# An MLP of seven block products: first product in 2 passes of 1024 tokens with stored operands, second without GpSimd in its loop

## The chip, the cores and the metric

One of the eight cores of a Trainium2 chip runs the kernel, one launch for the whole layer. The metric is the device time of one execution in microseconds, as the median over runs; lower is better. The engines are TensorE (PE, with its weight loads as PEld), VectorE (DVE), ScalarE (ACT), GpSimd (POOL) and SyncE (SP), which issues most transfers here.

## What is computed

The reference is one transformer layer over 2048 tokens of width 1024 (attention heads beside RWKV heads, an output projection, LayerNorm, then an MLP). The change lies in the MLP at the end and in what prepares it; cut to that:

```python
D_MODEL = 1024; SEQ = 2048; D_FF = 4 * D_MODEL

def squared_relu_mlp(h, w1, w2):
    return jnp.square(jax.nn.relu(h @ w1)) @ w2

    ...
    y = jnp.concatenate([y_na, y_rw], axis=-1) @ w_out
    x = layer_norm(ALPHA * x + g1 * y, ln1_g, ln1_b)
    x = layer_norm(ALPHA * x + g2 * squared_relu_mlp(modulate(x, sh2, sc2), mlp_w1, mlp_w2), ln2_g, ln2_b)
```

All values are float32.

## The kernel before

`phase1` and the first part of `tail` compute the two head groups; nothing changes there. Then come four stretches of `tail`.

**Opening.** `out_tiles` computes the output projection in 16 tiles of 128 tokens, with the first LayerNorm (`norm1`), and stores rows to X1 and their normalised form to XN in memory. The loop over the last tiles also calls `xstep`, which prepares the token side of the first product: it loads rows of XN (L1362), transposes them on TensorE (L1372), modulates them on ScalarE (L1375), forms block sums on VectorE (L1377 to L1380), and splits the result into a high part rounded to fp32r on ScalarE (L1382) and a low part on GpSimd (L1383). A step covers one of 4 slices of the width; four steps make the operands of 512 tokens. All steps use one tile `uk`.

**Split products.** A float32 product is taken as three fp32r products (high x high, high x low, low x high), so each operand is split into a rounded copy (ScalarE) and a rest (a subtraction, VectorE or GpSimd). On top of that a 2 x 2 block product is computed with 7 block products instead of 8, from sums of blocks. The 7 are numbered; products 1, 6, 7 and 4 of a group add up in one PSUM bank (a), 5 and 3 in another (b), 2 in a third.

**First product** (`mlp1`). Four passes of 512 tokens, the blocks being 256 tokens, 512 of the width and 128 hidden columns. A pass runs over 16 groups of 256 hidden columns, with 1 MB of weights per group loaded in each pass. A product is 12 matmuls of 256 columns (L1469). `prep` makes the weight side four products ahead: block sums (L1419 to L1425), high part (L1428), low part (L1429), all on ScalarE and VectorE. `seq` interleaves the products of two neighbouring groups. Behind the matmuls three results are copied (L1477) and three added to them (L1487); one instruction squares the group's 1024 columns (L1480), and the hidden values go to H in memory. At the end of a pass the operands of the next are split (L1491, L1492); `xstep` has made them during the pass.

**Second product** (`mlp2`). Two halves of 1024 tokens. A half runs over 7 groups of 512 hidden rows by the 7 products, and an eighth group that is computed with plain products. One of its units (a product of a group) is 24 matmuls of 512 columns (L1610). `load` reads H and the weights, `prep` makes block sums of both sides (S at L1550, T at L1557, on GpSimd but for a few at the start of a half) and `split` their parts (L1530: tokens on VectorE, weights on GpSimd or VectorE). Units are prepared two ahead. After each unit its four banks are added to `acc` (L1617; L1615 is the first copy). `std_prep` prepares the eighth group (GpSimd multiplies and splits its weights), and `mlp_end` computes it (L1679, L1681), combines it with X1 (L1662 on GpSimd for 6 of 8 rows, L1663), normalises and stores.

The order on each engine is that of a list scheduler which walks the program by priority of program order and lets later work pass where earlier work is not ready in its own simulation. Tiles share memory by tags with a number of buffers; a new tile waits for the last reader of the one whose place it takes. Pools of a stage that has ended give their memory to the next stage.

Of the kernel before, what the change touches and what calls it, by code (L numbers as in the profile page):

```python
# [15 lines left out]
D = 1024  # L16
# [26 lines left out]
M1LEAD = 4  # L43
M2LEAD = 2
FAST = (1, 5, 6, 3)
# [9 lines left out]
class Kern:  # L55
# [4 lines left out]
    def setup(self):  # L60
# [29 lines left out]
        self.H = scr("H", [32, 128, T])  # L90
# [709 lines left out]
    def tail(self):  # L800
        nc, tc, a = self.nc, self.tc, self.a
        ex = ExitStack()
        with ExitStack() as ep:
            with ExitStack() as eo:
# [57 lines left out]
                self.psN = self.pool(ep, "psN", 4, space=PSUM, side="right")  # L862
                self.xp = self.pool(ex, "xp", 1, side="right")
                self.xh = self.xp.tile([128, 7, 4, 256], F32R, name="xuh")
                self.xl = self.xp.tile([128, 7, 4, 256], F32R, name="xul")
                for i, _ in enumerate(tiles):
                    if i < 2:
                        self.xstep(0, 2 * i)
                        self.xstep(0, 2 * i + 1)
        with ExitStack() as em:  # L870
            self.base = self.pool(em, "base", 4)
            with ExitStack() as e1:
                self.mlp1(e1)
            ex.close()
            self.mlp2(em)

# [479 lines left out]
    def xstep(self, q, k, u=None):  # L1356
        nc = self.nc
        pool = self.xp
        t = pool.tile([128, 4, 2, 128], F32, name="xn", bufs=2)
        for j in range(4):  # L1360
            r = OB[2 * q + j // 2] + j % 2 * 128
            nc.sync.dma_start(t[:, j], self.XN[r:r + 128, :].rearrange("p (x k c) -> p x k c", x=2, c=128)[:, :, k, :])  # L1362
        if u is None:
            uk = pool.tile([128, 7, 256], F32, name="uk")
            at = [uk[:, i] for i in range(7)]
        else:
            at = [u[i // 2][:, i % 2, k * 256:k * 256 + 256] for i in range(7)]
        b12 = pool.tile([128, 256], F32, name="b12")
        for x, ds in enumerate(((at[0], b12), (at[1], at[2]))):
            ps = self.psN.tile([128, 512], F32, name="psn")  # L1370
            for j in range(4):
                nc.tensor.transpose(ps[:, j * 128:(j + 1) * 128], t[:, j, x, :], self.ident)  # L1372
            kk = 4 * x + k
            for c, d in enumerate(ds):
                nc.scalar.activation(d, ps[:, c * 256:c * 256 + 256], AF.Identity, bias=self.m2[:, 0, kk:kk + 1],  # L1375
                                     scale=self.m2[:, 1, kk:kk + 1])
        nc.vector.tensor_tensor(at[3], b12, at[0], ALU.subtract)  # L1377
        nc.vector.tensor_tensor(at[4], at[2], at[3], ALU.subtract)
        nc.vector.tensor_tensor(at[5], at[2], b12, ALU.subtract)
        nc.vector.tensor_tensor(at[6], at[1], at[4], ALU.subtract)  # L1380
        if u is None:
            nc.scalar.copy(self.xh[:, :, k, :], uk)  # L1382
            nc.gpsimd.tensor_tensor(self.xl[:, :, k, :], uk, f32(self.xh[:, :, k, :]), ALU.subtract)  # L1383


    def mlp1(self, es):
        nc, a = self.nc, self.a
        P = lambda name, **kw: self.pool(es, name, 1, **kw)
        up, sp, srcp, zp, pp = P("w1u"), P("w1sum"), P("w1src"), P("h1"), P("h1p")
        lp = P("l1c")  # L1390
# [5 lines left out]
        src, sums, units = {}, {}, {}  # L1396

        def load(g):
            if g < NG:
                if g < 2:  # L1400
                    t = self.base.tile([128, 2, 1024], F32, tag="c8", name="w10")
                    src[g] = t.rearrange("p a (k c) -> p (a k) c", k=4)
                else:
                    src[g] = srcp.tile([128, 8, 256], F32, name="w1", bufs=3)
                c = g % 16 * 256
                (nc.scalar if g < 2 else nc.sync).dma_start(src[g], a["mlp_w1"].rearrange("(k p) c -> p k c", p=128)[:, :, c:c + 256])

        def prep(n):
# [3 lines left out]
            w = src[g]  # L1412
            a11, a12, a21, a22 = [w[:, 4 * k:4 * k + 4, f * 128:f * 128 + 128] for f in range(2) for k in range(2)]
            if pr in (1, 2, 4):
                x = {1: a11, 2: a12, 4: a22}[pr]
            else:
                x = sums[g, pr] = sp.tile([128, 4, 128], F32, name="w1s", bufs=5)
                if pr == 5:
                    nc.vector.tensor_tensor(x, a21, a22, ALU.add)  # L1419
                elif pr == 6:  # L1420
                    nc.vector.tensor_tensor(x, sums.pop((g, 5)), a11, ALU.subtract)
                elif pr == 7:
                    nc.vector.tensor_tensor(x, a11, a21, ALU.subtract)
                else:
                    nc.vector.tensor_tensor(x, a12, sums.pop((g, 6)), ALU.subtract)  # L1425
            h = up.tile([128, 4, 128], F32R, tag="w1u", name="w1h", bufs=20)
            l = up.tile([128, 4, 128], F32R, tag="w1u", name="w1l", bufs=20)
            nc.scalar.copy(h, x)  # L1428
            nc.vector.tensor_tensor(l, x, f32(h), ALU.subtract)  # L1429
# [371 lines left out]
```

## Time and profile before

| | us |
|---|---|
| median of 3 runs | 3548.64 (3531.97 to 3555.44) |
| profiled execution, its own time | 3559.12 |
| its span, first to last instruction | 3557.3 |
| first product, about | 2161 to 2832 |
| second product, about | 2832 to 3557 |

The span is the time between the first and the last instruction of one profiled execution; the time of that execution lies 1.8 us above. Engine busy times are sums over instructions, and matmuls overlap, so TensorE's busy time is above the time that its matmuls occupy it. In a table of stretches PEclk is the share of TensorE's full clock that was granted.

### The profile page before, as it was taken

What the parts mean: (1) busy time and instruction counts of PE and PEld (TensorE: products, weight loads), DVE (VectorE), ACT (ScalarE), POOL (GpSimd) and SP (SyncE); (2) the same over time, 40 slices, a digit from 0 to 9 for tenths busy, and PEclk for the clock granted to TensorE, in tenths of its full rate; (3) what the DMA queues carried; (4) which work ended last, traced back from release to release, by engine and by line L of the source; (5) the groups of instructions that cost most, each with busy time, mean ns of one, the idle gap of its engine ahead of it and who ended that gap; (6) DMA issues with size and microseconds to landing.
All of it is one profiled execution on the core that took longest, in us unless ns stands there. A gap on an engine that the chain in (4) does not pass through costs nothing. (4 is left out here: it accounts for less than half of the span.)

```text
span 3557.3 us, 71137 instructions
## 1 busy us (share of the span) xinstructions
PE 3240.4 (91%) x27864; PEld 2749.8 (77%) x27864; DVE 2903.6 (82%) x5245; ACT 1630.7 (46%) x3201; POOL 1036.4 (29%) x715
## 2 busy tenths in 40 slices
PE   7999999899939988999979988999999999989987
PEld 4878898789836766777757768999999978767775
DVE  5568887879696667776578768999999789999998
ACT  4555565455414445454432123565655443344333
POOL 0000000000014444544343331000000077877785
PEclk9999999899969999999989989999999999999998
DMA  7487367546775555454364535555455423243322
GB/s 245 141 244 206 95 165 193 156 114 173 191 176 127 121 133 122 116 137 109 81 202 154 151 126 198 177 163 169 157 172 197 158 102 117 97 148 113 119 95 83
DMA packets 752291, 528.48 MB, mean 149 GB/s; under 512 B 376940, under 2 KB 671596, under 8 KB 751956
## 3 DMA queue, kind: packets, MB, share of 16 engines
q1 hardware_dynamic: 676586, 487.47, 47.1%
q10 hardware_dynamic: 75370, 36.46, 3.6%
q8 instruction: 220, 3.60, 0.4%
q14 instruction: 115, 0.94, 0.1%
HBM read 359.70 MB, written 164.11 MB: 147 GB/s over the span
## 5 line engine op out<-in xcount | busy, mean ns | idle before, releaser
L442 PE MATMUL psm<-xh,wh 128*128 128x386 f32 (+1 forms) x1104 | 380.4, 347 | 14.5 <-ACT row L445 10.3
L442 PE MATMUL psm<-xl,wh 128*128 128x386 f32 (+1 forms) x1104 | 380.4, 345 | 3.3 <-DVE xl L413 3.2
L442 PE MATMUL psm<-xh,wl 128*128 128x386 f32 (+1 forms) x1104 | 376.5, 341 | 0.0
L1530 POOL TENSOR_TENSOR ul<-wp,uh 128x1024 fp32r<-128x1024 f32 x50 | 142.3, 2850 | 733.2 <-ACT uh L1530 729.6
L1469 PE MATMUL psa<-xuh,w1l 128*128 128x256 f32 x1024 | 287.8, 283 | 9.1 <-DVE w1l L1429 8.9
L1469 PE MATMUL psa<-xuh,w1h 128*128 128x256 f32 x1024 | 290.0, 284 | 4.6 <-ACT p L1477 1.7
L1469 PE MATMUL psa<-xul,w1h 128*128 128x256 f32 x1024 | 288.1, 282 | 0.0
L442 PEld LDWEIGHTS psm<-xh,wh 128*128 128x128 f32 x1104 | 210.0, 191 | 40.7 <-ACT row L445 20.9
L442 PEld LDWEIGHTS psm<-xl,wh 128*128 128x128 f32 x1104 | 210.1, 190 | 17.9 <-issue 7.3
L442 PEld LDWEIGHTS psm<-xh,wl 128*128 128x128 f32 x1104 | 210.1, 190 | 5.0 <-issue 3.7
L1469 PEld LDWEIGHTS psa<-xuh,w1l 128*128 128x128 f32 x1024 | 193.2, 189 | 10.4 <-DVE w1l L1429 10.4
L1469 PEld LDWEIGHTS psa<-xuh,w1h 128*128 128x128 f32 x1024 | 193.8, 189 | 6.8 <-ACT p L1477 2.6
L1469 PEld LDWEIGHTS psa<-xul,w1h 128*128 128x128 f32 x1024 | 193.9, 189 | 0.0
L752 DVE TENSOR_TENSOR stmp<-mp,xp 128x9 f32<-128x9 f32 (+30 forms) x310 | 168.2, 543 | 24.3 <-DMA vw<-VN 7.4
L1428 ACT CAST w1h<-w1s 128x512 fp32r<-128x512 f32 x256 | 156.3, 622 | 67.6 <-PE psa L1469 25.1
L1429 DVE TENSOR_TENSOR w1l<-w1s,w1h 128x512 fp32r<-128x512 f32 x256 | 176.2, 698 | 8.7 <-ACT w1h L1428 8.2
L1610 PE MATMUL psqa<-ul,uh 128*128 128x512 f32 x400 | 162.7, 407 | 20.4 <-DVE ul L1530 18.3
L428 DVE TENSOR_TENSOR wl<-wst,wh 128x1024 fp32r<-128x1024 f32 x81 | 98.7, 1219 | 87.3 <-ACT wh L427 69.4
L1610 PE MATMUL psqa<-uh 128*128 128x512 f32 x400 | 154.1, 401 | 14.0 <-ACT uh L1530 7.2
L982 POOL TENSOR_SCALAR S<-S,mx 128x640 f32<-128x640 f32 (+1 forms) x128 | 106.0, 828 | 202.2 <-DVE mx L980 121.4
L1610 PE MATMUL psqb<-ul,uh 128*128 128x512 f32 x384 | 151.0, 393 | 11.7 <-DVE ul L1530 8.7
L1610 PE MATMUL psqa<-uh,ul 128*128 128x512 f32 x400 | 161.0, 402 | 0.0
(405 smaller groups left out, 10151.0 us busy)
## 6 DMA issues: line engine op xcount, KB each, us to landing
w<-in_mlp_w SPq DMA_DIRECT2D x62, 1024.0 KB
wst<-in_w_in SPq DMA_DIRECT2D x81, 512.0 KB
H<-h SPq DMA_DIRECT2D x64, 512.0 KB
hp<-H SPq DMA_DIRECT2D x32, 1024.0 KB
wp<-in_mlp_w SPq DMA_DIRECT2D x32, 1024.0 KB
wmod<-in_w_mod SPq DMA_DIRECT2D x48, 512.0 KB
bkc<-BK SPq DMA_DIRECT2D x36, 512.0 KB
AR<-ar SPq DMA_DIRECT2D x64, 256.0 KB
```

The source lines that it names most:

```text
L428: nc.vector.tensor_tensor(wl, w, f32(wh), ALU.subtract)
L442: nc.tensor.matmul(ps[:, :y - x], lhsT=s[:, k, :], rhs=m[:, k, x:y], start=(i == 0), stop=(i == 23))
L752: nc.vector.tensor_tensor(tv, mp[:, i:i + 1, lo:lo + n].to_broadcast([128, n, n]), xp[:, lo:lo + n, lo:lo + n], ALU.mult)
L982: nc.gpsimd.tensor_scalar(x, x, m[:, 6:7], 1.0, ALU.mult, ALU.mult)
L1428: nc.scalar.copy(h, x)
L1429: nc.vector.tensor_tensor(l, x, f32(h), ALU.subtract)
L1469: nc.tensor.matmul(ps, lhsT=w[:, k, :], rhs=x[:, xu[pr], k, :], start=(i == 0 and pr in (1, 5, 2)), stop=(i == 11), skip_group_check=True)
L1530: return (h, l), [lambda: nc.scalar.copy(h, x), lambda: eng.tensor_tensor(l, x, f32(h), ALU.subtract)]
L1610: nc.tensor.matmul(ps, lhsT=x[:, c, s], rhs=y[:, c, :], start=(i == 0 and new), stop=(i == 5), skip_group_check=True)
```

## The change

The first product is done in 2 passes of 1024 tokens with blocks of 512, so its matmuls have 512 columns and there are 32 groups; the products of a group run one after the other (`MORD`), the weight side is prepared three products ahead, and each weight block is loaded once per pass. The token operands of a pass are made in 8 steps of `xstep` (4 slices of the width by 2 halves of each token block). Before pass 1 the steps split three operands and store the other four to a buffer XU in memory, from which `mlp1` loads and splits them; the second pass's seven operands are all stored to XU by steps during the first pass and reloaded as the first pass's last group releases each tile. Splits of token operands are on VectorE, none on GpSimd.

After the matmuls `mlp1` squares the four blocks of a group separately, forms the block sums that the second product needs, and stores all seven operands to HU (for the last two blocks of each pass, which belong to the plain group, the four blocks alone). The second product loads one operand per unit, three units before it is prepared, and splits it in place. Weight differences are formed in place on VectorE. Its groups (`M2G`) are two units deep: two consecutive units of one product add up in the same PSUM banks and are then added to `acc` once. `std_prep` runs on VectorE and ScalarE. `mlp_end` itself is not changed.

The diff, cut to its core:

```diff
-M1LEAD = 4
+M1LEAD = 3
 M2LEAD = 2
-FAST = (1, 5, 6, 3)
+ALEAD = 3
+MORD = (1, 5, 6, 3, 7, 2, 4)
+XU = {pr: i for i, pr in enumerate(MORD)}
+M2G = ((0, 2), (4, 2), (8, 2), (12, 1))
+M2STD = 14
-        self.H = scr("H", [32, 128, T])
+        self.HU = scr("HU", [2, 16, 128, 7, 512])
+        self.XU = scr("XU", [2, 128, 7, 4, 512])
...
+                self.uk = self.base.tile([128, 8, 256], F32, tag="uk", name="uk")
...
+                self.w1load(0)
+                m = 0
                 for i, _ in enumerate(tiles):
-                    if i < 2:
-                        self.xstep(0, 2 * i)
-                        self.xstep(0, 2 * i + 1)
+                    for m in range(m, min(m + 3, 8)):
+                        self.xstep(0, m // 2, m % 2)
+                    m += m < 8
...
+    def xstep(self, q, k, c):
...
+        def keep(pr):
+            if q == 0:
+                h, l = self.xu[pr]
+                nc.scalar.copy(h[:, k, cs], x[pr])
+                V.tensor_tensor(l[:, k, cs], x[pr], f32(h[:, k, cs]), ALU.subtract)
...
+        V.tensor_tensor(x[4], x[2], x[6], ALU.subtract)
+        for pr in MORD[:3]:
+            keep(pr)
+        i = 3 if q == 0 else 0
+        nc.sync.dma_start(self.XU[q, :, i:7, k, cs], self.uk[:, i:7])
...
+    def w1load(self, g):
+        if g < 32:
+            pool, tag = (self.xp, "w1a") if g % 2 == 0 else (self.srcp, "w1b")
+            self.w1[g] = pool.tile([128, 8, 256], F32, tag=tag, name="w1")
+            c = g % 16 * 256
+            self.nc.sync.dma_start(self.w1[g], self.a["mlp_w1"].rearrange("(k p) c -> p k c", p=128)[:, :, c:c + 256])
...
     def mlp1(self, es):
-        NG = 64
-        seq = [(g + o, pr) for g in range(NG + 1) for o, pr in ((0, 1), (-1, 7), (0, 5), (-1, 3), (0, 6), (-1, 4), (0, 2))
-               if 0 <= g + o < NG]
+        NG = 32
+        seq = [(g, pr) for g in range(NG) for pr in MORD]
...
+        def xload(q, pr):
+            nc.sync.dma_start(f32(self.xu[pr][1]), self.XU[q, :, XU[pr]])
+        def xsplit(pr, src=None):
+            h, l = self.xu[pr]
+            src = f32(l) if src is None else src
+            nc.scalar.copy(h, src)
+            V.tensor_tensor(l, src, f32(h), ALU.subtract)
+        def square(z):
+            V.scalar_tensor_tensor(z, z, 0.0, z, ALU.max, ALU.mult)
+        for pr in MORD[3:]:
+            xload(0, pr)
+        self.w1load(1)
+        todo = {n + 1: [lambda pr=pr: xsplit(pr)] for n, pr in enumerate(MORD[3:])}
...
+            if g == 15:
+                if pr == 1:
+                    xsplit(1, u1)
+                else:
+                    xload(1, pr)
+                    todo.setdefault(n + 4, []).append(lambda pr=pr: xsplit(pr))
+            def out(z, u, q=q, fg=fg):
+                todo.setdefault(n + 1, []).append(lambda: nc.sync.dma_start(self.HU[q, fg, :, XU[u]], z))
...
+            elif pr == 7:
+                z12, z22 = st["p", 6], st["p", 5]
+                V.tensor_tensor(z22, ps, z22, ALU.add)
+                square(z22)
+                out(z22, 4)
+                if not std:
+                    s = st["s1"] = T("s1")
+                    V.tensor_tensor(s, z12, z22, ALU.add)
+                    out(s, 5)
...
     def mlp2(self, es):
+        def hload(half, fg, pr):
+            t = up.tile([128, 2, 512], F32R, tag="al", name="al", bufs=6)
+            nc.sync.dma_start(f32(t), self.HU[half, fg:fg + 2, :, XU[pr]].rearrange("c p t -> p c t"))
+            return t
...
+        seq = [(half, g, pr, kk) for half in range(2) for g in range(len(M2G)) for pr in MORD for kk in range(M2G[g][1])]
...
+            if y is not None:
+                fs.append(lambda: V.tensor_tensor(B, y, B, ALU.subtract))
+            al = hs.pop(n)
+            ah = u3("ah")
+            ub, fb = split(B)
+            units[n] = (ah, al), ub
+            fs += [lambda: nc.scalar.copy(ah, f32(al)), fb[0],
+                   lambda: V.tensor_tensor(al, f32(al), f32(ah), ALU.subtract), fb[1]]
...
-                new = pr in (1, 5, 2)
+                new = pr in (1, 5, 2) and kk == 0
...
+                if not end:
+                    pass
+                elif g == 0 and pr in (1, 5, 6, 4):
                     nc.scalar.copy(o, ps)
...
-        fs = [lambda w=w: nc.gpsimd.tensor_tensor(w, w, g2[:, None, :].to_broadcast([128, 2, D]), ALU.mult) for w in wp]
+        fs = [lambda w=w: nc.vector.tensor_tensor(w, w, g2[:, None, :].to_broadcast([128, 2, D]), ALU.mult) for w in ws]
```

## Rows read from the trace of the kernel before

**Rows 1.** The page, engine totals: busy time, share of the span, instructions.

```profile
PE 3240.4 (91%) x27864; PEld 2749.8 (77%) x27864; DVE 2903.6 (82%) x5245; ACT 1630.7 (46%) x3201; POOL 1036.4 (29%) x715
```

**Rows 2.** Table of stretches: start to end, length, busy time (and count) per engine.

```profile
core 0: us, PE busy (x) PEld busy (x) DVE busy (x) ACT busy (x) POOL busy (x), PEclk, DMA share, GB/s
2080.00:2160.00 80.00, 72.65 (x299) 53.54 (x297) 61.66 (x94) 23.05 (x41) 31.02 (x15) 0.91 0.36 115
2160.00:2230.00 70.00, 59.47 (x456) 58.27 (x457) 64.09 (x108) 34.83 (x75) 8.46 (x2) 0.90 0.59 201
2230.00:2832.00 602.00, 596.89 (x5014) 593.25 (x5012) 557.79 (x945) 342.62 (x704) 0.00 (x0) 1.00 0.52 169
2832.00:3112.00 280.00, 264.11 (x1126) 212.95 (x1127) 266.08 (x246) 105.73 (x114) 215.75 (x75) 0.98 0.33 117
3112.00:3215.00 103.00, 80.36 (x329) 63.58 (x328) 96.13 (x90) 51.44 (x77) 72.43 (x25) 0.92 0.42 151
3215.00:3478.00 263.00, 249.48 (x1067) 202.89 (x1067) 256.17 (x243) 97.51 (x102) 208.65 (x72) 0.97 0.29 105
3478.00:3558.00 80.00, 53.38 (x219) 42.84 (x217) 69.19 (x77) 24.43 (x41) 44.28 (x15) 0.86 0.20 79
```

**Rows 3.** Chain of waits: start, length, what, in each product.

```profile
2816.24 2.84 PE psa L1469 x24
...
2858.27 5.44 PE psqb L1610 x24
```

**Rows 4.** Table of stretches, matmul line of the first product alone.

```profile
2161.00:2832.00 671.00, 650.75 (x5376) 642.83 (x5376) 0.99 0.53 171
```

**Rows 5.** Second product: tile ul (minimum/median/maximum ns), then groups by line (busy us, mean ns).

```profile
L1530 DVE TENSOR_TENSOR ul<-S,uh x56: 1209/2196/3397, 2839.1 to 3459.3; 128x1024 fp32r<-128x1024 f32 x56
L1530 DVE TENSOR_TENSOR ul<-hp,uh x50: 1208/3052/5039, 2833.4 to 3499.4; 128x1024 fp32r<-128x1024 f32 x50
...
L1617 DVE TENSOR_TENSOR acc<-psqb,acc 128x512 f32<-128x512 f32 x184 | 119.1, 677 | 4.7 <-PE psqb L1610 4.7
```

**Rows 6.** First product: groups by line (busy us, mean ns).

```profile
L1429 DVE TENSOR_TENSOR w1l<-w1s,w1h 128x512 fp32r<-128x512 f32 x256 | 176.2, 698 | 8.7 <-ACT w1h L1428 8.2 <-PE psa L1469 0.2
L1428 ACT CAST w1h<-w 128x512 fp32r<-128x512 f32 x192 | 114.1, 622 | 41.6 <-PE psa L1469 18.0 <-DMA w<-in_mlp_w 16.6 <-PE pse L1469 3.1
...
L1480 DVE SCALAR_TENSOR_TENSOR h<-h 128x1024 f32<-128x1024 f32 x63 | 76.6, 1217 | 5.9 <-ACT h L1479 5.8
...
L1419 DVE TENSOR_TENSOR w1s<-w 128x512 f32<-128x512 f32 x64 | 43.7, 683 | 8.5 <-DMA w<-in_mlp_w 8.5
L1487 DVE TENSOR_TENSOR h<-pse,p 128x256 f32<-128x256 f32 x64 | 26.7, 418 | 9.8 <-ACT w1h L1428 4.0 <-PE pse L1469 3.3 <-ACT p L1477 1.4
```

**Rows 7.** Waits in the second product: us in total, times, longest.

```profile
ACT uh L1530 <- POOL S L1550: 201.3, 49, 7.8
...
PEld psqa L1610 <- DVE ul L1530: 22.8, 11, 4.8
```

**Rows 8.** Start of the first product: one stretch, one row of TensorE's timeline.

```profile
2160.00:2170.00 10.00, 2.40 (x11) 2.19 (x12) 4.29 (x7) 2.55 (x5) 0.00 (x0) 0.67 1.00 349
...
2168.11 0.58 PE L1469 MATMUL psa<-xuh,w1l 128*128 128x256 f32 x1 [6.41 <-DVE w1l L1429]
```

**Rows 9.** Opening: VectorE's timeline, groups of GpSimd and ScalarE, DMA issues (ns).

```profile
2088.18 0.35 DVE L1380 TENSOR_TENSOR uk<-uk 128x256 f32<-128x256 f32 x1
...
2130.34 0.41 DVE L1380 TENSOR_TENSOR uk<-uk 128x256 f32<-128x256 f32 x1
...
L1383 POOL TENSOR_TENSOR xul<-uk,xuh 128x1792 fp32r<-128x1792 f32 x4 | 16.2, 4050 | 36.9 <-ACT xuh L1382 36.9
...
L1375 ACT ACTIVATE u<-psn,m 128x256 f32<-128x256 f32 x36 | 19.3, 564 | 7.5 <-PE psn L1372 7.2
...
L1362 SPq DMA_DIRECT2D xn<-XN x64: 517/605/1222, 2070.6 to 2526.0; - x64
```

**Rows 10.** Last matmuls: first and last start of a line (us).

```profile
L1679 PE MATMUL psqb<-uh,ul x64: 388/389/389, 3146.6 to 3537.6; 128*128 128x512 f32 x64
```

More of the change, by code (lines that the diff above doesn't have):

```diff
@@ L1376, in xstep @@
                                      scale=self.m2[:, 1, kk:kk + 1])
[L1377 to L1383, printed above, removed]
+        V.tensor_tensor(x[5], at[7], x[1], ALU.subtract)
@@ L1408, in prep @@
+        seq = [(g, pr) for g in range(NG) for pr in MORD]
+        sums, units = {}, {}
         def prep(n):
@@ L1411, in prep @@
             g, pr = seq[n]
-            w = src[g]
+            w = self.w1[g]
             a11, a12, a21, a22 = [w[:, 4 * k:4 * k + 4, f * 128:f * 128 + 128] for f in range(2) for k in range(2)]
-            if pr in (1, 2, 4):
-                x = {1: a11, 2: a12, 4: a22}[pr]
[L1416 to L1425, printed above, removed]
@@ L1428, in prep @@
+            h = up.tile([128, 4, 128], F32R, tag="w1u", name="w1h", bufs=10)
+            l = up.tile([128, 4, 128], F32R, tag="w1u", name="w1l", bufs=10)
             nc.scalar.copy(h, x)
-            nc.vector.tensor_tensor(l, x, f32(h), ALU.subtract)
+            V.tensor_tensor(l, x, f32(h), ALU.subtract)
             units[n] = h, l
             if pr == 4:
-                load(g + 3)
-                del src[g]
-        for g in range(3):
-            load(g)
+                self.w1load(g + 2)
+                del self.w1[g]
@@ L1497, in mlp2 @@
+        for fs in todo.values():
+            for f in fs:
+                f()
     def mlp2(self, es):
@@ L1564, in mlp2 @@
-        NS = 7
-        seq = [(half, g, pr) for half in range(2) for g in range(NS) for pr in ORD]
-        srcs = {(0, 0): load(0, 0)}
-        sums = {}
-        units = {}
-        steps = []
-        def lead(n):
-            half, g, pr = seq[n]
-            if pr == ORD[0]:
-                sums.clear()
-            if pr == ORD[1]:
-                srcs[half, g + 1] = load(half, g + 1)
-            units[n], fs = prep(srcs[half, g], sums, pr, g == 0 and pr in FAST)
+            if cnt[0] % 7 == 1:
+                return self.base.tile([128, 2, 1024], F32, tag="uk", name=name)
@@ new lines, in split, with wloads @@
+        def split(x):
+            h, l = u3("uh"), u3("ul")
+            return (h, l), [lambda: nc.scalar.copy(h, x), lambda: nc.vector.tensor_tensor(l, x, f32(h), ALU.subtract)]
+        lo, hi = slice(0, 512), slice(512, 1024)
+        seq = [(half, g, pr, kk) for half in range(2) for g in range(len(M2G)) for pr in MORD for kk in range(M2G[g][1])]
+        ws, hs, units, banks, steps = {}, {}, {}, {}, []
+        def wloads(half, g):
+            if g == len(M2G):
+                return [lambda i=i: ws.__setitem__((half, g, 0, i), wload(M2STD, i)) for i in range(2)]
+            f0, nk = M2G[g]
+            return [lambda i=i, kk=kk: ws.__setitem__((half, g, kk, i), wload(f0 + 2 * kk, i))
+                    for i in range(2) for kk in range(nk)]
@@ L1584, in run @@
             del fs[:k]
+        for f in wloads(0, 0):
+            f()
+        for n in range(M2LEAD + ALEAD):
+            aload(n, 0)
         for n in range(M2LEAD):
@@ L1609, in mlp2 @@
                     for x, y in ((ah, bh), (ah, bl), (al, bh)):
-                        nc.tensor.matmul(ps, lhsT=x[:, c, s], rhs=y[:, c, :], start=(i == 0 and new), stop=(i == 5),
+                        nc.tensor.matmul(ps, lhsT=x[:, c, s], rhs=y[:, c, :], start=(i == 0 and new), stop=(i == 5 and end),
                                          skip_group_check=True)
```

295 lines of the change are left out of this document (160 added, 135 removed).

## Prediction

> **What bounds the kernel now.** I read the page's engine totals first: TensorE 91% busy, VectorE 82%, GpSimd 29% [rows 1]. These are means over stages, so next comes the table of stretches [rows 2]: the opening (last output tiles, first operand preparation) 2080 to 2160, the first product 2160 to 2832, the second 2832 to the end. Column two is TensorE; the reader is to hold it against VectorE. In the first product both are nearly full (596.89 and 557.79 of 602). In the second VectorE is full (266.08 of 280, 256.17 of 263) and TensorE is not.
>
> Busy matmul time overlaps itself, so I count matmuls and multiply by their spacing, which the chain of waits gives where it runs on TensorE alone: 24 matmuls of 256 columns in 2.84 us, 118.3 ns each; 24 of 512 columns in 5.44 us, 226.7 ns [rows 3]. The first product's 5376 [rows 4] need 636.0 us. The second's stretches hold 1126 + 329 + 1067 + 219 = 2741 matmuls [rows 2], or 621 us of 725.3: 104 us are lost there, namely 280 - 255.3 = 24.7, 103 - 74.6 = 28.4, 263 - 241.9 = 21.1 and 79.3 - 49.6 = 29.7.
>
> Why lost? The same vector instruction (low part of a split, 128x1024) takes from 1.21 to 5.04 us, median 2.2 or 3.1, in the second product, where GpSimd works beside it [rows 5]; at its least it costs what a 128x1024 vector instruction costs in the first product, 1.217 us, where GpSimd rests [rows 6]. The scalar casts wait 201.3 us for GpSimd's block sums, and TensorE's weight loads wait for the vector splits [rows 7]. So the second product is set by VectorE, slowed by GpSimd.
>
> **First product: what changes.** Each of 32 groups (2 passes x 16) does 7 products x 12 matmuls of 512 columns: 2688 matmuls, half of before, each twice as wide. 2688 x 226.7 = 609.4 us, 26.6 less.
>
> The Trainium skill, "TensorE: Matmul & The Clock Gate", section "Back-to-back issue gap", speaks against this: it gives an isolated gap of N/2.4 + 2.5 ns, by which 5376 x 109.2 against 2688 x 215.8 would save only 7 us. Rows 3 show 118.3 and 226.7 instead, so the rows decide.
>
> Vector work per group: 4 sums of weights and 7 low parts, as before, 128x512 at 0.68 to 0.70 us: 4 x 0.683 + 7 x 0.69 = 7.6. Behind the matmuls before: 3 adds of 256 columns and one square of 1024, 3 x 0.418 + 1.217 = 2.5; in all 10.0 us against TensorE's 84 x 118.3 = 9.9 [rows 3, 6]. After, per group of twice the tokens: 3 adds, 3 squares, 4 subtractions (the block sums that GpSimd made later) of 512 columns, 10 x 0.68 = 6.8; in all 14.4 against 84 x 226.7 = 19.0. So 28 of 32 groups leave VectorE a quarter free; the last two blocks of each pass store 4 operands and do less. Scalar work stays far below (7 casts, 3 copies, 2 activations, each at most the 0.622 of a cast: 7.5 of 19.0) [rows 6].
>
> Transfers: 212 stores of 256 KB (28 groups x 7 + 4 x 4) for 64 of 512 KB, 32 weight loads for 64. That is 56 MB + 34 MB, with 22 MB of token operands written and read: 112 MB in some 640 us, 175 GB/s, beside 169 now and 349 at the peak [rows 2, 8]. Costed at nothing: weight loads come a whole group (19 us) ahead. If that cover were gone, 1 MB at 349 GB/s is 3 us per group. The stores are queued on SP in the order of the products, where they can hold a weight load only by the few us that a result is late.
>
> Losses inside: before, counting transposes as matmuls, 70 - 456 x 0.1183 = 16.1 at the start and 602 - 5014 x 0.1183 = 8.8 later [rows 2]. The start loss is a weight split that TensorE awaits 6.4 us [rows 8]. After, 4 MB of operands are reloaded and split there: from below nothing (they are used at products 4 to 7 and a split, 2.4 us, is about a product, 2.7), from above 4.2 MB / 349 GB/s = 12 us. I take 2 more than now. At the change of pass (one, for three before) six 1 MB loads and splits fall into 19 us; vector work there is 14.4 + 7 x 2.4 = 31 for 19, less the lead of three products (8): 0 to 15, I take 6, and 3 less for the older changes. Of 96 transposes 64 stay (-3.8). Sum: -26.6 + 2 + 6 - 3 - 3.8 = -25.
>
> **Opening.** Pass 1 now needs eight operand steps before its first matmul instead of four. The four of before end on VectorE 14 us apart (2088.2 to 2130.3), each behind a 4.05 us GpSimd split [rows 9]. All use one tile, which now is also stored before it is rewritten. From above: the eighth ends at 2088 + 7 x 14 = 2186, 26 beyond the first matmul now at about 2160. From below: 7 vector instructions of 0.42, 4 activations of 0.564, 3 casts and a store, some 8 us, end at 2080 + 64 = 2144, hidden behind the output tiles. VectorE has 80 - 61.66 = 18 us free in the opening [rows 2] and gets 8 x 2.9 - 4 x 1.7 = 17 more, but GpSimd's 16.2 us, which slow it, go. 32 row loads at 0.605 us of SP's time instead of 16 add 10 us to a queue that also feeds the output tiles [rows 9]. Between: six steps done when the output tiles end, two more at 7: +12.
>
> **Second product.** The matmuls stay (98 units x 24, plus 384). Block sums of the token side are gone from it. Vector work per unit: 2 low parts and 4/7 weight differences, 2.57 x 1.217 = 3.1; the adds out of PSUM fall since two units share a bank (96 per half instead of 180): 96 x 0.677 / 49 = 1.3 [rows 5]. Sum 4.5 against TensorE's 5.44. TensorE becomes the bound, so the losses inside the halves go: 24.7 to 8 (the tiles at the start reuse the first product's memory), 21.1 to 3. In the last 7 units of a half nothing is shared: 3.1 + 2.7 = 5.8 per unit, then the last block's preparation, on VectorE now (2 x 2.4 + 8 x 1.217 = 14.6), of which 9.7 must end before the plain products; the two units before give 10.9. So 5 to 8 us of stall stays per half. GpSimd keeps the multiplications of the end rows. I take 28.4 to 18, and 29.7 to 26, of which 19.3 are after the last matmul [rows 10]. New operand loads, 0.5 MB per unit of 5.44 us, with weights some 140 GB/s, are issued three units ahead: hidden; without that cover about 1.5 us per unit. Sum: 104 - 55 = 49 saved.
>
> **Sum.** 25 - 12 + 49 = 62 us. The profiled execution took 3559.1 us (span 3557.3), so its like would take 3497. The runs shown have their median 10.5 us lower, at 3548.6: forecast 3487.
>
> **Rivals.**
> *Operand staging is late* (0.14): the opening pays 26 instead of 12, the start's reload 12 instead of 2, the change of pass 15 instead of 6. 3487 + 14 + 10 + 9 = 3520. For it: one tile for eight steps. Against: GpSimd's 4 us per step go.
> *The spacing belongs to the stage, not to the width* (0.04): no 26.6, so 3514. Against: the two spacings lie on one line with 10 ns fixed.
> *VectorE holds the first product's banks* (slower, 0.12): product 4 adds into the bank from which VectorE must first read product 7, with only product 2 (2.7 us) between; before, three products lay between. If VectorE reads 3 us later than that in each of 32 groups, 97 us are lost: 3487 + 97 = 3584, 1% slower. Below 1.9 us per group (62 / 32) it is no slower. Against: VectorE's 75% load.
> *More is won* (0.08): opening and change of pass hidden, 8 us less at the ends: 3487 - 12 - 6 - 8 = 3461.
> Also, were the slow vector instructions not GpSimd's doing, they would stay at about 2.2 and a unit would cost 7.0; that is 3487 + 98 x 1.5 = 3634, but the 1.21 minima deny it, and it is within the 0.12.
>
> **How the numbers follow.** Forecast 0.62, its own range 3455 to 3513. About 1% (35 us) is what a measurement of this kernel can tell from no change. Faster: 0.62 + 0.08 = 0.70. Same: 0.14 + 0.04 = 0.18. Slower: 0.12. The range leaves out the slower case and the far ends of the first rival and the fourth: 3450 to 3535.
>
> **What would show it.** Right: first-product matmuls 227 ns apart and VectorE at most 85% there; second product with vector splits at 1.22 us, TensorE gaps only at the halves' ends, GpSimd idle outside them. Wrong: the first matmul of the first product later than 2190, gaps there each group that end on a vector add, or casts waiting for operand loads.

## The result, and the profile after

The changed kernel took 3504.9 us in its first measurement (3497.3 to 3507.8), against 3546.5 of the kernel before on the same chip: ratio 0.988 (0.985 to 0.992). Measured again beside the last experiments it took 3496.4 against 3551.2: 0.985 (0.983 to 0.986). It is faster, by 1.2 to 1.5%. The forecast was 3487, its range 3450 to 3535. Between the medians the gain is 41.6 and 54.8 us; between the two profiles, of which that of before (3559) is slower than the runs beside it, it is 52.6 behind the output tiles.

Below, stages are counted from the start of the last matmul of the output tiles (line 1338 of the changed kernel, 1324 of the one before), because the part ahead of it moves by up to 14 us between the profiles. It stands at 2159.0 in the profile of before and at 2160.2 in that of after.

| us after the last output-tile matmul | before | after | forecast of the difference |
|---|---|---|---|
| first matmul of the first product | 2.2 | 19.8 | +12 |
| last matmul of the first product | 672.5 | 669.0 | -13 |
| end of the span | 1398.3 | 1345.7 | -62 |

So the opening and the first product together gave 3.5 us where 13 were forecast, and the second product 49.1 (725.8 to 676.7) where 49 were. The forecast for the second product is met to the microsecond, and that is partly luck, as the stretches show. The table of stretches of after (start to end, length, then busy time and count of each engine, granted clock, DMA share, GB/s) answers [rows 2]:

```profile
2160.00:2180.00 20.00, 0.64 (x3) 0.19 (x1) 6.68 (x13) 4.21 (x7) 0.00 (x0) 0.59 0.95 315
2180.00:2420.00 240.00, 229.46 (x994) 182.41 (x995) 175.96 (x288) 96.07 (x173) 8.41 (x2) 0.98 0.63 207
2420.00:2829.30 409.30, 407.05 (x1760) 329.34 (x1758) 285.39 (x430) 153.71 (x255) 0.00 (x0) 1.00 0.47 157
2829.30:2852.00 22.70, 0.49 (x3) 0.17 (x2) 1.13 (x1) 3.44 (x5) 0.00 (x0) 0.57 1.02 388
2852.00:3110.00 258.00, 258.00 (x1130) 213.41 (x1131) 208.28 (x217) 112.58 (x118) 0.00 (x0) 0.99 0.48 156
3110.00:3180.00 70.00, 61.67 (x264) 50.00 (x263) 65.21 (x75) 33.05 (x51) 35.14 (x12) 0.96 0.45 162
3180.00:3430.00 250.00, 250.00 (x1103) 206.98 (x1102) 204.89 (x220) 111.46 (x121) 3.03 (x1) 1.00 0.49 163
3430.00:3506.00 76.00, 55.43 (x244) 45.23 (x242) 62.14 (x79) 25.70 (x41) 37.49 (x12) 0.88 0.16 62
```

The first, third and fifth busy times (TensorE, VectorE, GpSimd) tell the story. Inside the halves of the second product TensorE is busy throughout (258.00 of 258, 250.00 of 250), VectorE 81 to 82% and GpSimd all but silent (0 and 3.03 us); before, VectorE was full there and TensorE was not. But two stretches are almost empty of matmuls: 20 us ahead of the first product and 23 us ahead of the second, both with the DMA engines full (0.95 and 1.02, at 315 and 388 GB/s) and a granted clock of 0.59 and 0.57, near the lower of its two levels (1.2 GHz), while TensorE does next to nothing.

The waits of TensorE from 2160 to 2852 (who waited, for whom: total us, times, longest) name the two:

```profile
PE psqa L1699 <- ACT uh L1610: 22.2, 1, 22.2
PE psa L1513 <- ACT w1h L1452: 19.7, 2, 19.4
PE psa L1513 <- DVE p L1539: 5.4, 5, 1.5
PE psb L1513 <- DVE w1l L1453: 2.4, 1, 2.4
```

The third row is the slower rival (VectorE still reads a bank that the next product adds into). It exists, and it costs 5.4 us in the whole first product, not 97.

The chain of waits in the first product of after answers [rows 3] (start, length, what):

```profile
2803.71 5.55 PE psa L1513 x24
2809.25 2.80 PE psb L1513 x12
2812.05 2.75 PE psa L1513 x12
2814.80 2.72 PE pse L1513 x12
```

Twelve matmuls of 512 columns take 2.80 us in three of the products (1, 5 and 6), 233 ns each, and 2.72 in product 2, 227 each. The three products that run right behind a slow one take 2.75 (5.55 for 24 is one of each). It is the same in every group where nothing waits. A group of 84 takes 19.36 us where nothing waits (19.87 before for the same work, 168 x 118.3), not the 84 x 226.7 = 19.04 of the forecast.

The vector instructions of the second product answer [rows 5] (stretch 2852 to 3110; busy us, mean ns, idle before):

```profile
L1610 DVE TENSOR_TENSOR ul<-wp,uh 128x1024 fp32r<-128x1024 f32 x51 | 62.1, 1218 | 4.9 <-ACT uh L1610 4.8
L1655 DVE TENSOR_TENSOR al<-al,ah 128x1024 fp32r<-128x1024 f32 x49 | 59.9, 1223 | 62.5 <-ACT ah L1654 62.3
L1708 DVE TENSOR_TENSOR acc<-psqb,acc 128x512 f32<-128x512 f32 x45 | 29.6, 683 | 0.1
```

The low parts cost 1.22 us, as forecast.

### The profile page after: what moved, and what is told of

Read it like the earlier page. It is cut to its first block, busy times and chain, and to the rows that moved or that the text cites. A ratio compares the mean times of both kernels' runs of the same rounds, so it can differ in the third digit from the quotient of the medians.

```text
span 3506.0 us, 65269 instructions
## 1 busy us (share of the span) xinstructions
PE 3204.8 (91%) x25176; PEld 2608.2 (74%) x25176; DVE 2606.6 (74%) x4891; ACT 1522.6 (43%) x2891; POOL 553.2 (16%) x551
## 5 line engine op out<-in xcount | busy, mean ns | idle before, releaser
L449 PE MATMUL psm<-xh,wh 128*128 128x386 f32 (+1 forms) x1104 | 380.5, 347 | 16.0 <-ACT row L452 10.2
L1513 PE MATMUL psa<-xh,w1h 128*128 128x512 f32 x512 | 203.8, 398 | 25.9 <-ACT w1h L1452 19.7
L1513 PE MATMUL psa<-xl,w1h 128*128 128x512 f32 x512 | 202.1, 395 | 0.0
L1513 PE MATMUL psa<-xh,w1l 128*128 128x512 f32 x512 | 201.0, 393 | 0.3 <-DVE w1l L1453 0.3
L1655 DVE TENSOR_TENSOR al<-al,ah 128x1024 fp32r<-128x1024 f32 x98 | 120.7, 1231 | 100.1 <-ACT ah L1654 99.9
L1699 PE MATMUL psqa<-uh,ah 128*128 128x512 f32 x400 | 156.9, 395 | 29.3 <-ACT uh L1610 22.2
L759 DVE TENSOR_TENSOR stmp<-mp,xp 128x9 f32<-128x9 f32 (+30 forms) x310 | 167.4, 540 | 20.9 <-DMA mp<-LB 8.9
L1699 PE MATMUL psqa<-ul,ah 128*128 128x512 f32 x400 | 156.9, 392 | 0.0
L1699 PE MATMUL psqa<-uh,al 128*128 128x512 f32 x400 | 156.6, 392 | 0.0
L760 DVE TENSOR_REDUCE xp<-stmp 128x3 f32<-128x9 f32 (+30 forms) x310 | 153.9, 497 | 3.4
L1699 PE MATMUL psqb<-ul,ah 128*128 128x512 f32 x384 | 149.4, 389 | 0.0
L1699 PE MATMUL psqb<-uh,al 128*128 128x512 f32 x384 | 149.4, 389 | 0.0
```

The costliest lines, as they stand in the source:

```text
L449: nc.tensor.matmul(ps[:, :y - x], lhsT=s[:, k, :], rhs=m[:, k, x:y], start=(i == 0), stop=(i == 23))
L759: nc.vector.tensor_tensor(tv, mp[:, i:i + 1, lo:lo + n].to_broadcast([128, n, n]), xp[:, lo:lo + n, lo:lo + n], ALU.mult)
L760: nc.vector.tensor_reduce(xp[:, lo:lo + n, i], tv, AX.X, ALU.add)
L1513: nc.tensor.matmul(ps, lhsT=w[:, k, :], rhs=x[:, k, :], start=(i == 0 and pr in (1, 5, 2)), stop=(i == 11), skip_group_check=True)
L1655: lambda: V.tensor_tensor(al, f32(al), f32(ah), ALU.subtract), fb[1]]
L1699: nc.tensor.matmul(ps, lhsT=x[:, c, s], rhs=y[:, c, :], start=(i == 0 and new), stop=(i == 5 and end), skip_group_check=True)
```

## Experiments

All start from the changed kernel, except e4_before_shift_32. Line numbers in a run's rows are those of its own kernel, so one and the same line moves by a few. Ratios are against the kernel before on the same chip, with 95% intervals; the changed kernel's own ratios are 0.988 and 0.985. Each run also has a profile, read stage by stage as above.

### The gap ahead of the second product: e1_operands_first

SP's queue of after, at the change of products (start, us in issue, what, count), shows six weight blocks of 1 MB issued ahead of the first token operand:

```profile
2828.12 1.70 SPq L1600 DMA_DIRECT2D wp<-in_mlp_w  x2
2830.95 0.34 SPq L1525 DMA_DIRECT2D HU<-z  x1
2831.40 2.21 SPq L1600 DMA_DIRECT2D wp<-in_mlp_w  x4
2833.67 12.64 SPq L1605 DMA_DIRECT2D al<-HU  x6
```

```diff
-        for f in wloads(0, 0):
-            f()
-        for n in range(M2LEAD + ALEAD):
+        first = wloads(0, 0)
+        first[0]()
+        aload(0, 0)
+        behind(first[1])
+        aload(1, 0)
+        behind(first[2])
+        aload(2, 0)
+        behind(first[3])
+        for n in range(3, M2LEAD + ALEAD):
             aload(n, 0)
...
-                        f()
+                        behind(f) if (half, g) == (0, 0) else f()
```

> Changed kernel, with the loads at the start of the second product in another order on SP's queue: one block of weights, the first token operand, then weights and operands in turn, and the second group's weights only behind the operands (in the changed kernel six weight blocks of 1 MB stand ahead of the first operand). Theory (the 22.6 us gap of TensorE from 2829.2 is the first operand waiting behind 6 MB): the gap falls to 8 to 10 us, the run to about 13 us less than the changed kernel (3492). Rival 1 (the operand's memory or the last stores of the first product release it): gap and time stay, 3505. Rival 2 (the weights are then late in their turn): the gap falls, but gaps of several us appear in the next 25 us, and under 5 us is saved.

Measured: 3482.4 us, ratio 0.980 (0.978 to 0.982). TensorE's wait there, in this kernel's waits:

```profile
PE psqa L1710 <- ACT uh L1615: 8.3, 1, 8.3
```

The gap between the two products is 8.7 us instead of 22.6, and the end comes 1333.8 us after the last output tile, 11.9 earlier. No new gap follows. The theory holds: the first operand's 0.5 MB waited behind 6 MB. With the right order the start costs about the 8 us that the prediction had put down for it.

### The gap ahead of the first product: e2_weights_first and e8_last_store_first

ScalarE's timeline of after (start, us, what, idle before and its releaser) shows the first weight cast behind the split of a reloaded operand that only the fourth product uses:

```profile
2177.55 1.90 ACT L1465 CAST xh<-xl 128x2048 fp32r<-128x2048 f32 x1 [12.96 <-DMA xl<-XU]
2179.35 0.61 ACT L1452 CAST w1h<-w 128x512 fp32r<-128x512 f32 x1
```

The run sets an order on ScalarE and VectorE: each operand's split issues behind the casts, low parts and PSUM copies that come earlier in the work (listed by unit in `made`).

```diff
+        def behind(n, f):
+            with ExitStack() as s:
+                for i in made[n]:
+                    s.enter_context(self.tc.issue_after(i))
+                f()
...
-        todo = {n + 1: [lambda pr=pr: xsplit(pr)] for n, pr in enumerate(MORD[3:])}
+        todo = {n + 2: [lambda n=n, pr=pr: behind(n + 3, lambda: xsplit(pr, n=n))] for n, pr in enumerate(MORD[3:])}
...
-                    self.norm1(x, slice(r, r + 128), xn, rows[:, 0], rows[:, 1], osm)
+                    behind(3, lambda: self.norm1(x, slice(r, r + 128), xn, rows[:, 0], rows[:, 1], osm))
```

> Changed kernel, with an order set at the start of the first product: ScalarE's casts and VectorE's low parts of the first weights, and the copies of the first products out of PSUM, stand ahead of the split of the four reloaded token operands; the sum of the second group's weights and the last rows' normalization stand behind the first four low parts. Theory (the 19.8 us gap before the first matmul is ScalarE waiting for a reloaded operand at the head of its queue, which products 1, 5 and 6 do not need): the first matmul comes at 2167 to 2170 instead of 2180.0, and three products fit before the fourth waits for its operand until about 2180; 6 to 10 us saved, about 3497. Rival (the last operand steps, which end at 2167, or the weights set the start): first matmul at 2178 or later, nothing saved. Rival 2 (the reload of 4 MB is itself the bound): the first matmul comes early, but the end of the first group stays where it is, at about 2200, and nothing is saved.

Measured: 3499.5 us, ratio 0.986 (0.985 to 0.988): no gain. The first matmul came 5.0 us after the last output tile, but that of the second unit (product 5 of the first group) only at 22.8, and the whole first product ended at 669.4 (669.0 in after). The waits of ScalarE from 2149 to 2170 say why:

```profile
ACT w1h L1459 <- DMA X<-xres: 13.4, 1, 13.4
```

The high part of the second unit's weights takes the memory of the last output tile, whose store has not landed. SP's queue shows that store (X<-xres) behind a load that itself waits for another store:

```profile
2155.84 0.37 SPq L1403 DMA_DIRECT2D XU<-uk  x1
2156.27 0.50 SPq L1411 DMA_DIRECT2D w<-in_mlp_w  x1
2159.56 0.33 SPq L1468 DMA_DIRECT2D xl<-XU  x1
2159.99 0.38 SPq L1346 DMA_DIRECT2D X<-xres  x1
```

VectorE had finished that tile at 2156.7. So my theory of this gap was half of it: the order on ScalarE hid a second wait of nearly the same length. The next run keeps that order and moves that store (`lastx`) ahead of the reload; "the run before last" in its expectation is e2_weights_first.

```diff
+        with self.tc.issue_after(self.lastx):
+            for pr in MORD[3:]:
+                last = xload(0, pr)
+        with self.tc.issue_after(last.ins):
+            self.w1load(1)
```

> The order of the run before last on the opening (weights of the first product ahead of the reloaded operands on ScalarE and VectorE), and also on SP's queue: the store of the last output tile stands ahead of the reload of the token operands, and the second group's weights and the normalization's rows behind it. There the first matmul came 5 us after the last output tile, but the second weight tile waited until 18.4 us after it for that store, whose tile's memory it takes and which stood behind a load that waits for another store. Theory: the second product starts 9 to 12 us after the last output tile instead of 19, the first group ends some 10 us earlier than in the changed kernel (37 us after the last output tile instead of 47.8). Whether these 10 us last: theory says yes, 3495. Rival (the stores and vector work of the first groups set the pace): the groups behind take longer and time stays at 3500.

Measured: 3499.6 us, ratio 0.986 (0.984 to 0.988). The second unit now starts at 15.3 and the first group ends at 36.9 us (47.8 in after), but the next groups take 26.1 and 21.9 us (20.4 and 20.5), and the first product ends at 666.5: of 10.9 us gained, 2.5 are left. The stretches of this run show VectorE (the third busy time) 83 to 92% busy meanwhile, and ScalarE's waits from 2170 to 2230 show what the weight casts, for which TensorE waits, wait for themselves:

```profile
2170.00:2190.00 20.00, 17.45 (x66) 13.21 (x66) 18.41 (x18) 10.27 (x11) 4.32 (x1) 0.91 0.63 238
2190.00:2210.00 20.00, 15.82 (x59) 12.49 (x58) 16.67 (x31) 7.09 (x14) 0.86 (x1) 0.83 0.63 224
2210.00:2230.00 20.00, 18.08 (x78) 14.10 (x77) 17.81 (x27) 6.46 (x13) 1.92 (x1) 1.00 0.46 149
```

```profile
ACT w1h L1459 <- DVE w1s L1448: 16.7, 2, 11.0
```

In the stretch where TensorE does least (59 matmuls) VectorE is not full, but the weight sums (`w1s`) had stood behind its splits and the normalization: one cast waited 11.0 us for them. The rival holds as far as vector work goes: a gap at a start is not time to be had when another engine's work waits behind it.

### The spacing of matmuls: e3_shift_32, e4_before_shift_32, e6_shift_480, e5_halves_of_256

The token operands are the `rhs` of these matmuls. Their addresses follow from the order of the tiles in the program; the profiles hold none. In after those of products 1, 5 and 6 begin at byte 155616 of each partition and then every 8192 bytes, 480 past a multiple of 512; those of the other four begin at multiples of 512. In before all began 480 past a multiple.

```diff
-                        rows = self.base.tile([128, 2, 1024], F32, tag="uk", name="l1gb")
+                        rows = self.base.tile([128, 2056], F32, tag="uk", name="l1gb")
+                        rows = rows[:, :2048].rearrange("p (a b) -> p a b", a=2)
```

> Changed kernel, with one vector tile made 32 bytes longer, so that the six token operands of products 1, 5 and 6 lie 32 bytes lower in SBUF (byte 155584 instead of 155616 in each partition, now a multiple of 64 as the other operands' addresses are); nothing else changes. Theory (the matmuls of products 1, 5 and 6 are 234 ns apart and the others 227 because of that address): 227 in all products, about 4 ns less on 2688 matmuls in the mean, 9 to 13 us less, 3494. Rival (they are slower for where they stand in the order, or for a bank of PSUM): 234 stays and 3505.

Measured: 3494.4 us, ratio 0.985 (0.983 to 0.987), like the changed kernel. The products stay slow (here product 1, then 3, chain of waits):

```profile
2780.65 2.80 PE psa L1514 x12
2783.45 2.74 PE psb L1514 x12
```

The same shift in the kernel before:

```diff
-        b12 = pool.tile([128, 256], F32, name="b12")
+        b12 = pool.tile([128, 264], F32, name="b12")[:, :256]
```

> Kernel before, with one tile 32 bytes longer, so that all token operands of the first product (256 columns wide there) lie 32 bytes lower, at a multiple of 64. Theory (part of what the prediction put down to the width was the address): spacing of the 5376 matmuls of 256 columns falls from 118.3 to 114 to 116 ns where TensorE runs on its own, and up to 16 us are saved, less what VectorE (93% busy there) takes back; the widening is then worth only some 5 to 12 us and not 26.6. Rival (the width alone): 118.3 stays, time stays at 3548.

Measured: 3529.9 us, ratio 0.994 (0.992 to 0.996), for 32 bytes. The chain of waits, where [rows 3] have 2.84 for 24:

```profile
2765.22 2.72 PE psa L1469 x24
```

113.3 ns each, exactly half of the 226.7 of 512 columns. So where this pace holds, the 10 ns that the prediction read as fixed per matmul are gone with 32 bytes of address. It does not hold throughout. For most of the second pass, from one gap of TensorE to another (some 114 us), the same matmuls at the same addresses ran some 118 ns apart (stretch, matmul line alone):

```profile
2380.00:2490.00 110.00, 110.00 (x936) 110.00 (x935) 1.00 0.53 172
```

The address is therefore not the whole of it. The same 32 bytes left the 512-column products slow, so 64 bytes could not be the boundary. The next run used 480 (a tile of 2168 elements in place of 2056).

> Changed kernel, with one vector tile 480 bytes longer, so that the operands of products 1, 5 and 6 begin at a multiple of 512 bytes in each partition, as those of the other four do (32 bytes lower changed only the pattern of their spacing, not its mean of 233.4 ns). Theory (a row of 2 KB that begins off a coarser boundary than 64 bytes costs 6 ns more): 227 in all seven products, 19.04 us for a group of 84 where nothing waits instead of 19.36, 10 us less in all. Rival (something else about these three products, the place in SBUF above 150 KB or the order): 233 stays.

Measured: 3487.1 us, ratio 0.983 (0.981 to 0.985). All products run at one pace:

```profile
2780.53 2.72 PE psb L1514 x12
2783.25 5.44 PE psa L1514 x24
```

A group takes 19.04 us where nothing waits, and the first product ends at 657.1 instead of 669.0. The products behind the slow ones, 2.75 in after, are at 2.72 too. The longer tile also changed the order at the start (the first matmul came at 4.0 us), but it did the same in e3, where the spacing stayed and the first product ended at 665.2. So of the 11.9 us about 8 are spacing and about 4 came with the order.

Last, the width alone, in the changed kernel:

```diff
-                    nc.tensor.matmul(ps, lhsT=w[:, k, :], rhs=x[:, k, :], start=(i == 0 and pr in (1, 5, 2)),
-                                     stop=(i == 11), skip_group_check=True)
+                    for c in (0, 256):
+                        nc.tensor.matmul(ps[:, c:c + 256], lhsT=w[:, k, :], rhs=x[:, k, c:c + 256],
+                                         start=(i == 0 and c == 0 and pr in (1, 5, 2)), stop=(i == 11),
+                                         skip_group_check=True)
```

> Changed kernel, with each matmul of the first product issued as two of 256 columns into the two halves of the same bank: 5376 matmuls again, all else as in the changed kernel. The prediction's step (a matmul has some 10 ns fixed, so half as many save 26.6 us): pairs take 2 x 118 ns where one took 227 to 234, and the run takes 13 to 25 us longer than the changed kernel. Theory after the shift of the kernel before (256 columns cost exactly half of 512): products 3, 7, 2 and 4 at 113 to 114 ns each, the products' total unchanged, time within 5 us of 3505. Products 1, 5 and 6: 113 to 117.

Measured: 3511.8 us, ratio 0.990 (0.988 to 0.992). My theory of "exactly half" fell: product 2, whose operand begins at a multiple of 512, takes 2.87 us as 24 halves, 119 to 120 ns each, against 2.72 as 12 whole ones (first row; the second is product 6, at 480 past a multiple, 118 each).

```profile
2795.66 2.87 PE pse L1514 x24
2798.52 2.84 PE psa L1514 x24
```

The first product is 661.1 us long instead of 649.2: here the width is worth 12 us. A group where nothing waits takes 20.0 us, 0.64 more; that would be 20 us in 32 groups, but the early groups are above this pace in either kernel. Both readings are true in their place. Beginning at a multiple of 512 bytes, 512 columns take 226.7 ns and two halves 2 x 119 to 120; beginning 448 past one, 233.3 and mostly 2 x 113.3; beginning 480 past one, 233.4 and 2 x 118.3. What the rule behind it is, these four runs do not settle, and the stretch of e4 at 118 shows that something besides the address enters.

### GpSimd beside VectorE: e7_gpsimd_beside

```diff
+            if n < 60:
+                nc.gpsimd.tensor_tensor(idle, g2, g2, ALU.subtract)
```

> Changed kernel, with 60 extra subtractions of 128x1024 on GpSimd during the second product, of a constant tile into a tile that nobody reads: VectorE's and ScalarE's work is as in the changed kernel. The prediction's step (the low parts on VectorE took 2.2 to 3.1 us before because GpSimd worked beside them, and not for a cause of their own): in the stretch where GpSimd is busy the low parts rise from 1.23 us to 2 us or more, VectorE goes from 80% to nearly full, a unit takes 6 us or more instead of 5.44, and the run is 20 to 90 us longer; behind that stretch all is as before. Rival (VectorE was slow for another reason): low parts stay at 1.23 and the time at 3505.

Measured: 3550.7 us, ratio 1.000 (0.998 to 1.002): 60 instructions that nobody waits for take back the whole gain of the change. VectorE's groups while GpSimd is busy (2845 to 2995):

```profile
L1611 DVE TENSOR_TENSOR ul<-wp,uh 128x1024 fp32r<-128x1024 f32 x20 | 51.8, 2591 | 0.0
L1656 DVE TENSOR_TENSOR al<-al,ah 128x1024 fp32r<-128x1024 f32 x20 | 49.2, 2458 | 2.7 <-ACT ah L1655 2.7
L1711 DVE TENSOR_TENSOR acc<-psqb,acc 128x512 f32<-128x512 f32 x12 | 7.9, 678 | 0.0
```

GpSimd's own in the same stretch:

```profile
L1687 POOL TENSOR_TENSOR idle<-g 128x1024 f32<-128x1024 f32 x50 | 138.0, 2760 | 3.9
```

And VectorE's behind it (3000 to 3150):

```profile
L1611 DVE TENSOR_TENSOR ul<-wp,uh 128x1024 fp32r<-128x1024 f32 x29 | 35.2, 1215 | 1.9 <-ACT uh L1611 1.9
```

A subtraction of two tiles takes 2.5 us beside GpSimd and 1.22 without it, and then VectorE is full (147 us of 150) and TensorE busy for only 115.5. The additions out of PSUM, one of whose inputs is no SBUF tile, stay at 0.68. The Trainium skill, "SBUF — State Buffer", section "SBUF: two separate sides", says that a VectorE instruction with two SBUF inputs and a GpSimd instruction that reads SBUF exclude each other for the whole instruction; this trace agrees (2.5 beside 1.22, and 0.68 unchanged).

### Two units in one bank: e10_no_sharing, beside e9_changed_again

```diff
-M2G = ((0, 2), (4, 2), (8, 2), (12, 1))
+M2G = tuple((f, 1) for f in range(0, 14, 2))
...
-                        wloads(1, 0)[3]()
+                        for f in wloads(1, 0)[3:]:
+                            f()
```

> The changed kernel itself, for a ratio on the same chip beside the three that follow: about 3500 to 3505, that is 0.987 to 0.989 of the kernel before.

Measured: 3496.4 us, ratio 0.985 (0.983 to 0.986); its stages are those of the first profile within 2 us (first product 670.8, end 1346.6).

> Changed kernel, with groups of 512 rows of the second product throughout: no two units share a bank, so each unit's four results are added out of PSUM (180 such additions per half instead of 96, at some 0.68 us). The prediction's step (VectorE's work per unit would be 5.8 us against TensorE's 5.44): 0.3 to 0.4 us lost in each of 84 units, 25 to 35 us longer than the changed kernel, VectorE over 95% busy in the second product and TensorE waiting for it. Rival (VectorE's fifth of free time takes the additions): within 5 us, VectorE at 90 to 95%.

Measured: 3509.4 us, ratio 0.988 (0.987 to 0.990): 13 us more than e9 in the times, 9 in the profiles. Its stretches inside the halves:

```profile
2855.00:3115.00 260.00, 259.31 (x1143) 214.41 (x1142) 250.96 (x300) 107.18 (x116) 0.00 (x0) 1.00 0.46 152
3215.00:3440.00 225.00, 224.00 (x987) 184.88 (x986) 221.22 (x269) 85.08 (x86) 0.00 (x0) 1.00 0.46 152
```

VectorE is 97 to 98% busy, and TensorE still hardly waits (0.7 and 1.0 us): most of the loss lies at the ends of the halves. The prediction's 5.8 us of VectorE per unit was too much, because vector instructions overlap: in the timelines one of 0.68 us is followed by the next 0.60 later (2186.27, 2186.87, 2187.47 in e8). 300 instructions took 251 us here; priced one by one with the prediction's durations, 126 x 1.217, 172 x 0.677 and 2 of 2.29, they are 274. So the sharing that I counted as needed is worth 9 to 13 us, not 30.

### Together: e11_two_mends and e12_three_mends

> The first run's order of loads at the start of the second product (a gap of 8.7 us there instead of 22.6) and the longer tile that puts the operands of products 1, 5 and 6 at a multiple of 512 bytes (19.0 us for a group instead of 19.36), together. Theory (they lie in different stages and add): 20 to 24 us less than the changed kernel, about 3480. Rival (one of them takes from the other): under 15 us.

Measured: 3476.8 us, ratio 0.979 (0.978 to 0.981). The first product ends at 656.9, the gap behind it is 8.7 us, the end comes at 1320.6, 26 earlier than in e9. The two add.

The last run adds e8's order and moves the normalization of the last 256 rows by two groups:

```diff
-                if g < 2:
+                if 2 <= g < 4:
```

> The two of the run before, the order of the opening with the last store first, and the normalization of the last 256 rows moved from the first two groups of the first product to the third and fourth. With the order of the opening alone the first group ended 10.9 us earlier, and the next two took 26.1 and 21.9 us instead of 20.4 and 20.5, with VectorE 83 to 92% busy. Theory (VectorE's work of those groups, 12 us of it the normalization, takes the gain back): the first group ends at about 37 us behind the last output tile, the next two take 19.5 to 20.5 us each, and 6 to 10 us more are saved than by the run before. Rival (the four splits of operands alone, 9 us, or the loads of weights set it): no more than 3 us.

Measured: 3471.9 us, ratio 0.977 (0.976 to 0.978), the fastest of all; in the profile the end comes at 1318.2, 2.4 earlier than in e11, so the difference between these two is small. The first group ends at 35.1 us (39.2 in e11), the next take 21.5 and 23.9 (22.8 and 20.9). The rival was nearer: no more than 3 us were saved, and the third group, to which the normalization had moved, took 3 us longer. Less vector work in the first four groups might free that time; it was not tried.

## Why the prediction came out as it did

**What bounds the kernel** was right. e7 puts the old bound back on its own: GpSimd beside VectorE, and the gain is gone.

**Second product, -49.** The sum was right and its parts were not. Counting matmuls at 226.7 ns as before, the losses of after are 22.5 + 1.8 = 24.3 in the first half (forecast 8), 10.2 between the halves (18), nothing in the second half (3) and 20.7 at the end (26): 55.2 against 55. The start was the step that failed. The prediction spoke of tiles that reuse memory there; it did not list what SP would issue first, 6 MB of weights ahead of 0.5 MB that TensorE needed (e1). What paid for it is, as far as e10 shows, the vector work, priced some 9% too high by adding durations: inside the halves TensorE lost no more than the 1.8 us at the first start, and the stalls of 5 to 8 us that were put at the last units of each half came to some 1.5 and 0.4.

**First product, -25.** Measured from its first to its last matmul it fell by 21.1 us: 16.3 from the spacing (32 x 0.51), 4.8 from everything else, where +1 was forecast. The change of pass, put at 6, cost 2.3 (four groups of 19.6, 20.7, 19.4 and 20.1 us). More was lost in groups 2 to 12, beside which the last rows' normalization and the second pass's operand steps run: 20.0 to 22.4 us each, 17.7 above the pace of 19.36 together, 64 transposes among it. The failed step is the widening's 26.6, of which 16.3 came. Its two rows were measured right and read wrong: [rows 3] come from operands that begin at different addresses, and the difference between 2 x 118.3 and 226.7 was put down to the width alone. The rival that the spacing belongs to the stage, given 0.04, was the one to look at: addresses differ by stage. The rule of the Trainium skill that was set against it ("TensorE: Matmul & The Clock Gate", section "Back-to-back issue gap") would have had the widening save 7 us, by the prediction's estimate; measured in place, by e5, it is 12. With good addresses on both sides, e4 and e6, the first product ends at 654.7 us in the old form and at 657.1 in the new one. So with these addresses the rewriting of the first product into 2 passes saves nothing by itself; all the gain is the second product's (726.3 to 678.2 in those two).

**Opening, +12.** It was +17.6. The steps themselves were forecast well enough: six were done in time and the last ended at 2167.0, 7 us after the output tiles. Then came what the prediction had put into another term at 2 us: the reload of 4 MB, at the head of ScalarE's queue, and on SP's queue ahead of the store that frees the weights' memory. Yet e8 shows that most of this stall hides vector work that has to be done anyway, so as a cost it is nearer 3 us than 18.

**Rivals.** Operand staging was late in the opening, as the first rival had it, for 6 us where it said 14; at the change of pass it was not. VectorE holding banks cost 5.4 us, not 97, at 70 to 73% load.

## What to carry to other kernels

A spacing read from one place in a trace holds for that operand's address too: before pricing a change of width by two rows, look at where in SBUF each operand begins, and try the address alone, which here cost one line and was worth 8 to 18 us of the first product. For every start of a stage, write out the queue that feeds it in issue order with its megabytes ahead of the first thing needed. And an empty stretch of one engine is worth only what the next fullest engine has free around it.

## What the runs showed of the hardware

- Moving a matmul's `rhs` operand in SBUF by 32 to 480 bytes changed the spacing of fp32r matmuls: 512 columns in 226.7 ns beginning at a multiple of 512 bytes (e6), 233.3 to 233.5 beginning 448 or 480 past one (e3, after); 256 columns mostly in 113.3 at 448 past, with a stretch of 114 us at 118 (e4), 118.3 at 480 past (before), 119 to 120 as halves of operands at multiples of 512 (e5). The rule behind it stays open.
- A subtraction of two SBUF tiles on VectorE (128x1024) takes 2.5 us instead of 1.22 while GpSimd works on SBUF tiles; an addition out of PSUM stays at 0.68.
- In the gap ahead of the second product, with TensorE idle, transfers ran at 388 GB/s over 22.7 us, above the 349 that the prediction took as the peak.
- Vector instructions overlap: 128x512 ones that last 0.68 us each started 0.60 apart (e8).
